# Dilated attention heads of a transformer kernel: outputs stored in two parts instead of one

## The chip, the cores and the metric

The kernel runs on one core of a Trainium2 chip. The metric is the device time of one execution in microseconds. Engines are named as the profile names them: PE is the matrix engine (TensorE), PEld its weight loads, DVE is VectorE, ACT is ScalarE, POOL is GpSimd, SP is SyncE. L902 is line 902 of the kernel.

## What is computed

A sequence of 1024 tokens with 1024 features goes through two blocks. The first block has a convolution layer and then a dilated attention layer, each with an adaptive normalisation ahead and a gated residual behind; the second has a sparse attention layer (indexer, top 256 of the keys, latent keys and values) and a convolutional feed-forward layer. The change lies in the dilated attention layer:

```python
def dilated_mixer(h, w_in, w_out, cos, sin):
    q, k, v, z = jnp.split(h @ w_in, [G * E, 2 * G * E, 2 * G * E + E], axis=-1)
    ...
    for g in range(G):        # rates 1, 4, 16
        ...
        o, lse = banded_attention(to_strided(q[:, :, g], r)[:, :, :, None], ...)
    wts = jax.nn.softmax(jnp.stack(lses, axis=0), axis=0)
    o = jnp.sum(wts[..., None] * jnp.stack(outs, axis=0), axis=0)
    y = o.reshape(B, S, E).astype(h.dtype) * jax.nn.silu(z)
    return y @ w_out
```

There are 8 heads of 128 features; `y @ w_out` is the out-projection.

## The kernel before, in words

Everything lies transposed, features on the 128 partitions and tokens along the free dimension, in two chunks of 512 tokens (`CH(c)`). Every matmul operand is kept as two numbers: `hi`, the value rounded to the matmul type float32r, and `lo`, the rest. A product takes three matmuls (`mm3`, and `gemm` for a block of 128 features): hi x hi, hi x lo, lo x hi. `split` (L381 to L385) makes the two from a float32 tile: a copy on ACT (L384) and a subtraction on DVE, or on another engine if one is named (L385). `weight` (L364 to L379) loads a block of weights from DRAM (L376) and makes its two parts on ACT (L377) and POOL (L378) into a ring of three pairs (`wring`), or loads ready parts (L372). `weight_own` (L666 to L673) does the same with buffers of its own.

The SBUF is handed out by `Arena`: pages, each of which holds at a time either float32 buffers or buffers of the rounded type (`ar.new(n, True)`; `new2` gives a pair of these). `new` prefers the buffers that were freed longest ago. A buffer that was given back may be in use still; whoever writes it next waits for its last reader. Nearly all loads and stores go through one in-order queue, that of SP (`dma`). The order of instructions on each engine comes from a scheduler: it follows the program's order as a priority and moves an instruction ahead where its simulated timeline has an engine free.

The dilated layer runs the heads one after another (loop at L948). A head projects queries and keys for three rates (`block`, L754; `rotate`, L733 to L749, which reads the projections from PSUM on ACT, L736 and L737, and DVE, L740), loads its values (L972), projects the gate `z`, and calls `attend` (L758 to L911). In between, `later.go()` prepares weights of later layers: load, split, and store as two parts (L353 to L358). `attend` makes scores and exponentials (L774 to L797), brings the row maxima and sums of the rates together by an exchange through a DRAM buffer (stores L810 to L812, loads L815 and L819; a transposition L817; weights L827 to L847), transposes the weighted scores with PE (`turned`: L857, split at L859 and L860) and multiplies them with the values. At the end of a head, for each chunk, DVE adds the last part (L902) and multiplies by the gate (L903) into a buffer `y`. For heads 0 to 6 `y` is stored to the DRAM tensor `yscr` as float32 (L908). For head 7 it is split at once and stays in SBUF (`Yc`, L905 and L906).

After the heads, `load_y` (L999 to L1007) loads for a chunk the seven stored outputs (L1004) and splits each (L1006), the subtraction on DVE for even heads and on POOL for odd ones. `finish_layer1` runs the out-projection of a chunk (`outproj`, L675 to L691: eight blocks of weights `w1o`, each a `gemm` over the eight heads in order, then the residual loaded at L685 and added at L686), and the norms behind it. Block 3 of chunk 0 has weights of its own buffers (L668 to L670). The calls stand at L1067 to L1072: `load_y` of chunk 0, five blocks of its out-projection, `load_y` of chunk 1, the rest. The scheduler mixes these loads, splits and matmuls with the end of head 7.

`load_y` serves two other layers as well (sources `yscr2` and `gscr`); those are single DRAM tensors.

Of the kernel before, what the change touches and what calls it, by code (L numbers as in the profile page):

```python
# [15 lines left out]
S = 1024  # L16
# [184 lines left out]
def emit(tc, I, OUT):  # L201
# [9 lines left out]
    dma = nc.sync.dma_start  # L211
# [4 lines left out]
    with sp as sp, pp as pp, dp as dp:  # L216
# [11 lines left out]
        def dram(shape, dtype=F32):  # L228
            serial[0] += 1
            return dp.tile(list(shape), dtype, name=f"d{serial[0]}")  # L230
# [150 lines left out]
        def split(hi, lo, src, hi_buf_f=None, engine=None):  # L381

            n = src.shape[-1]
            A.activation(hi.r[:, :n], src, AF.Copy)  # L384
            (engine or V).tensor_sub(lo.r[:, :n], src, hi.f[:, :n])  # L385
# [22 lines left out]
        def new2(n=512):  # L408
            return ar.new(n, True), ar.new(n, True)
# [71 lines left out]
        CH = lambda c: slice(512 * c, 512 * c + 512)  # L481
# [44 lines left out]
        Y = [[None, None] for _ in range(8)]  # L526
# [200 lines left out]
            dma(mask1[i].f, I["mask1"][:, 768 * i:768 * i + 768])  # L727
        m0 = [mask1[0].f[:, 256 * i:256 * i + 256] for i in range(3)]
        m12 = [mask1[1].f[:, 384 * i:384 * i + 384] for i in range(2)]
        yscr = dram([8, 128, S])  # L730
        Yc = [[None, None] for _ in range(8)]

        def rotate(p, c, out):  # L733
# [24 lines left out]
        def attend(h, q, k, vs, sz):  # L758
# [122 lines left out]
            def banded(i):  # L881

                s0 = lambda J, kk: S0[J // 2].f[:, 256 * (J % 2) + 128 * kk:
                                                256 * (J % 2) + 128 * kk + 128]
                pt = turned([s0((i - 1) % 8, 1), s0(i, 0), s0(i + 1, 1), s0(i + 2, 0)])
                p = psum("ps")
                for a in range(2):
                    tl = slice(256 * a, 256 * a + 256)
                    mm3(p[:, tl], v0(i + 2 * a), tuple(v[:, tl] for v in rr(pt)), True, True)
                for b in pt:  # L890
                    b.free()
                return p
# [6 lines left out]
            for c in range(2):  # L899
                p = banded(4 * c + 1)  # L900
                y = ar.new(512)
                V.tensor_tensor(nj(y.f), nj(p), ov[:, 64 * c:64 * c + 64], op=OP.add)  # L902
                V.scalar_tensor_tensor(y.f, y.f, 0.5, sz.f[:, CH(c)], op0=OP.mult, op1=OP.mult)  # L903
                if h == HEADS - 1:
                    Yc[h][c] = new2()  # L905
                    split(*Yc[h][c], y.f)  # L906
                else:
                    dma(yscr[h, :, CH(c)], y.f)  # L908
                y.free()
            for b in [*vs[0], *vs[1], *S0, *S1, o12, sz]:  # L910
                b.free()  # L911

# [35 lines left out]
        for h in range(HEADS):  # L948
            q = [new2(S), new2(S), (ar.new(S),)]
            k = [new2(S + 128), new2(S), (ar.new(S),)]  # L950
# [3 lines left out]
            for g in range(3):  # L954
                for t, off, pad in ((q, 0, 0), (k, 24, 64)):
                    p = block(off + 8 * g + h)
                    later.go()
                    for c in range(2):
# [5 lines left out]
                        b = t[g]  # L964
# [13 lines left out]
            for c in range(2):  # L978
                A.activation(sz.f[:, CH(c)], p[c], AF.Tanh, scale=0.5)
                V.scalar_tensor_tensor(sz.f[:, CH(c)], sz.f[:, CH(c)], 1.0, p[c], op0=OP.add,  # L980
                                       op1=OP.mult)
            attend(h, q, k, vs, sz)
        later.finish()
        for b in rope + mask1:
# [14 lines left out]
        def load_y(src, Y, c):  # L999
            for k in range(len(Y)):  # L1000
                if Y[k][c] is not None:
                    continue
                y = ar.new(512)
                dma(y.f, src[k, :, CH(c)])  # L1004
                Y[k][c] = new2()
                split(*Y[k][c], y.f, engine=G if k % 2 else V)  # L1006
                y.free()  # L1007

        def finish_layer1(c):
# [54 lines left out]
            if c == 1:  # L1064
                spare.free()

        load_y(yscr, Yc, 0)  # L1067
        ends1 = [finish_layer1(c) for c in range(2)]
        take(ends1[0], 5)
        load_y(yscr, Yc, 1)  # L1070
        drive(ends1[0])
        take(ends1[1], 6)  # L1072
# [402 lines left out]
        def finish_dsa(c, rest=()):  # L1475
            load_y(yscr2, Y2, c)
            acc = ar.new(512)
            xs = []

            def each(k, x):  # L1480
                square_sum(acc, x.f, k)
                xs.append(x)

            drive(outproj(prepared["w2o"], Y2, c, mods[:, 64:72], XF, X3, each))
            free_h(Y2, c)
            with tc.issue_after(lastn[3].ins):
                for _ in rest:
                    pass
            norm_h(xs, acc, s3, mods[:, 72:80], H3, c)
# [182 lines left out]
```

## Time and profile before

| | us |
|---|---|
| median of 3 runs | 2719.55 |
| the runs | 2713.51, 2719.55, 2720.99 |
| the profiled execution | 2724.1 |
| its span, first to last instruction | 2722.3 |
| mean granted clock of PE | 0.981 |

The profile is one execution. In it PE is busy for 95% of the span, DVE for 56%, ACT for 41%, POOL for 37%. A wait is put down to the instruction that released it. A matmul's duration includes its pipelined end, so durations of a run of matmuls overlap. "x12" counts instructions in a merged row. The granted clock is 1.00 at 2.4 GHz and 0.5 at 1.2 GHz. The heads lie at about 600 to 1406 us; head 0's last output is made at 740 us, head 6's at 1329, head 7's at 1409; the out-projection is under way from about 1377.

### The profile page before, as it was taken

How to read it: one execution, taken by the hardware profiler on the slowest of the kernel's cores; microseconds unless marked ns; L12 is line 12 of the kernel's file. 1: busy time of each engine (PE TensorE's matmuls, PEld its weight loads, DVE VectorE, ACT ScalarE, POOL GpSimd, SP SyncE). 2: the span in 40 equal slices, each digit the busy share in tenths (PEclk: the TensorE clock that was granted, in tenths of full speed). 3: DMA queues.
4: the chain of work that ended last, by engine and by line, in shares of the span. 5: the costliest groups of instructions: out<-in, count | busy, mean ns of one | idle time of the engine just before them, and what ended most of it. 6: DMA issues, size and time to landing. Idle time of an engine off the chain costs nothing. (4 is left out here: it accounts for less than half of the span.)

```text
span 2722.3 us, 34072 instructions
## 1 busy us (share of the span) xinstructions
PE 2588.6 (95%) x12070; PEld 2136.3 (78%) x12070; DVE 1528.9 (56%) x3260; ACT 1128.4 (41%) x1940; POOL 1009.8 (37%) x770
## 2 busy tenths in 40 slices
PE   8998999899999999999989888999999989999998
PEld 7876888788888788888867666777788868888887
DVE  7687532423756656665676699999555450222311
ACT  4211333414545445545443657784444442111132
POOL 1122236506446446536546335213111165200153
PEclk9999999999999999999999999999999999999999
DMA  7477765565444344444335674786566853676642
GB/s 296 156 260 258 261 222 193 166 199 171 166 163 170 139 163 171 149 170 172 132 122 182 212 248 117 248 269 225 192 203 212 273 194 107 210 256 245 224 122 74
DMA packets 208582, 524.67 MB, mean 193 GB/s; under 512 B 22258, under 2 KB 82202, under 8 KB 192796
## 3 DMA queue, kind: packets, MB, share of 16 engines
q1 hardware_dynamic: 199052, 497.20, 53.3%
q0 software_dynamic: 9216, 25.17, 3.1%
q8 instruction: 95, 1.56, 0.2%
q14 instruction: 75, 0.61, 0.1%
q10 hardware_dynamic: 144, 0.14, 0.0%
HBM read 394.03 MB, written 129.97 MB: 192 GB/s over the span
## 5 line engine op out<-in xcount | busy, mean ns | idle before, releaser
L256 PE MATMUL p<-page,wring 128*128 128x512 f32 (+2 forms) x8586 | 2017.9, 393 | 42.2 <-DVE page L572 11.5
L256 PEld LDWEIGHTS p<-page,wring 128*128 128x128 f32 (+1 forms) x8586 | 1602.0, 189 | 388.5 <-issue 10.4
L256 PE MATMUL p<-page,page 128*128 128x512 f32 (+5 forms) x2816 | 578.2, 349 | 64.9 <-DVE page L860 12.6
L378 POOL TENSOR_TENSOR wring<-wraw,wring 128x1024 fp32r<-128x1024 f32 (+1 forms) x159 | 387.9, 2440 | 551.6 <-ACT wring L377 479.6
L256 PEld LDWEIGHTS p<-page,page 128*128 128x128 f32 (+1 forms) x2816 | 461.8, 197 | 151.4 <-issue 18.4
L377 ACT ACTIVATE wring<-wraw 128x1024 fp32r<-128x1024 f32 (+1 forms) x159 | 164.6, 1036 | 301.0 <-PE p L256 272.7
L385 POOL TENSOR_TENSOR page<-page,page 128x512 fp32r<-128x512 f32 (+1 forms) x87 | 131.3, 1518 | 394.5 <-ACT page L384 369.6
L384 ACT ACTIVATE page<-page 128x512 fp32r<-128x512 f32 (+1 forms) x136 | 86.7, 651 | 178.3 <-DMA page<-d 69.8
L738 POOL TENSOR_TENSOR page<-page,page 128x512 f32<-128x512 f32 x96 | 125.4, 1310 | 71.4 <-ACT page L737 69.5
L355 DVE TENSOR_TENSOR wraw<-wraw,page 128x1024 fp32r<-128x1024 f32 (+1 forms) x64 | 78.8, 1231 | 126.4 <-ACT page L354 122.2
L301 DVE SCALAR_TENSOR_TENSOR page<-page,page 128x1024 f32<-128x1024 f32 x88 | 126.2, 1436 | 40.2 <-DMA page<-wmod 39.9
L747 POOL TENSOR_TENSOR page<-page,page 128x512 fp32r<-128x512 f32 x64 | 103.7, 1622 | 61.8 <-ACT page L746 61.6
L354 ACT ACTIVATE page<-wraw 128x1024 fp32r<-128x1024 f32 (+1 forms) x64 | 67.4, 1053 | 142.8 <-DMA wraw<-w3i 40.9
L1544 DVE SCALAR_TENSOR_TENSOR page<-p,page,page 128x512 f32<-128x512 f32 (+1 forms) x17 | 12.2, 719 | 202.9 <-PE p L256 202.9
L740 DVE TENSOR_TENSOR page<-p,page 128x512 f32<-128x512 f32 x96 | 66.1, 689 | 78.5 <-ACT page L737 73.1
L745 DVE TENSOR_TENSOR page<-page 128x512 f32<-128x512 f32 x64 | 95.4, 1492 | 25.6 <-POOL page L738 25.6
L1268 ACT ACTIVATE page<-page,page 128x1024 bf16<-128x1024 f32 (+1 forms) x93 | 86.9, 934 | 39.7 <-DVE page L1291 35.7
L746 ACT ACTIVATE page<-page 128x512 fp32r<-128x512 f32 x64 | 57.2, 894 | 75.7 <-DVE page L745 75.5
L736 ACT ACTIVATE page<-p 64x512 f32<-64x512 f32 x96 | 57.3, 596 | 72.4 <-PE p L256 54.1
L686 DVE SCALAR_TENSOR_TENSOR page<-p,page,page 128x512 f32<-128x512 f32 x48 | 35.9, 748 | 90.4 <-PE p L256 89.9
L1511 ACT ACTIVATE page<-p 128x512 f32<-128x512 f32 x44 | 26.2, 596 | 142.2 <-PE p L256 142.2
L441 POOL TENSOR_TENSOR page<-page,page 128x512 f32<-128x512 f32 x38 | 50.3, 1323 | 89.8 <-ACT page L440 89.8
(215 smaller groups left out, 2344.7 us busy)
## 6 DMA issues: line engine op xcount, KB each, us to landing
wring<-d SPq DMA_DIRECT2D x122, 1024.0 KB, 5.4
d<-page SPq DMA_DIRECT2D x95, 512.0 KB, 2.7
page<-wmod SPq DMA_DIRECT2D x88, 512.0 KB, 4.6
d<-page SPq DMA_DIRECT2D x153, 256.0 KB, 3.7
d<-wraw SPq DMA_DIRECT2D x63, 512.0 KB, 2.8
page<-d SPq DMA_DIRECT2D x121, 256.0 KB, 3.5
wraw<-w1i SPq DMA_DIRECT2D x56, 512.0 KB, 3.3
wraw<-w3i SPq DMA_DIRECT2D x44, 512.0 KB, 4.1
```

The lines of the kernel that those rows point to most:

```text
L256: lastn["mm"] = T.matmul(out, lhsT=l, rhs=r, start=start, stop=stop)
L301: V.scalar_tensor_tensor(w.f, w.f, 1.0, sil[j // 6].f, op0=OP.mult, op1=OP.mult, accum_out=m)
L354: A.activation(hi.r[:, :n], raw.f[:, :n], AF.Copy)
L355: V.tensor_sub(raw.r[:, :n], raw.f[:, :n], hi.f[:, :n])
L377: A.activation(hi.r[:, :n], raw.f[:, :n], AF.Copy)
L378: (lo_engine or G).tensor_sub(lo.r[:, :n], raw.f[:, :n], hi.f[:, :n])
L384: A.activation(hi.r[:, :n], src, AF.Copy)
L385: (engine or V).tensor_sub(lo.r[:, :n], src, hi.f[:, :n])
L738: G.tensor_mul(sw.f, sw.f, rope[1].f[:, CH(c)])
L745: V.tensor_tensor(a.f, a.f, sw.f, op=OP.add)
L747: G.tensor_sub(out[1], shape(a.f), out[2])
L1268: A.activation(junk.b[:, 0:sc.n], sc.f, AF.Sign, scale=-1.0, bias=at, accum_out=one)
```

## The change

`yscr` becomes a list of two DRAM tensors. At the end of every head `y` is split (ACT and DVE) and given back at once; head 7 keeps its parts as before, heads 0 to 6 store both parts, each a transfer of 128 x 512 float32 (256 KB). `load_y`, when its source is a list, loads the two parts directly into a pair of rounded buffers and does no split. The other two uses of `load_y` are as before.

```diff
-        yscr = dram([8, 128, S])
+        yscr = [dram([8, 128, S]) for _ in range(2)]
...
                 V.scalar_tensor_tensor(y.f, y.f, 0.5, sz.f[:, CH(c)], op0=OP.mult, op1=OP.mult)
+                parts = new2()
+                split(*parts, y.f)
+                y.free()
                 if h == HEADS - 1:
-                    Yc[h][c] = new2()
-                    split(*Yc[h][c], y.f)
-                else:
-                    dma(yscr[h, :, CH(c)], y.f)
-                y.free()
+                    Yc[h][c] = parts
+                    continue
+                for b, out in zip(parts, yscr):
+                    dma(out[h, :, CH(c)], b.f)
+                    b.free()
...
         def load_y(src, Y, c):
             for k in range(len(Y)):
                 if Y[k][c] is not None:
+                    continue
+                if isinstance(src, list):
+                    Y[k][c] = new2()
+                    for b, part in zip(Y[k][c], src):
+                        dma(b.f, part[k, :, CH(c)])
                     continue
                 y = ar.new(512)
                 dma(y.f, src[k, :, CH(c)])
```

## Rows read from the trace of the kernel before

**Rows 1.** The page: busy time, share, instructions of each engine.

```profile
PE 2588.6 (95%) x12070; PEld 2136.3 (78%) x12070; DVE 1528.9 (56%) x3260; ACT 1128.4 (41%) x1940; POOL 1009.8 (37%) x770
```

**Rows 2.** Waits of PE from 700 to 1340: total us, times, longest.

```profile
PE p L256 <- DVE page L860: 10.8, 6, 4.4
PE p L256 <- DVE page L740: 7.1, 7, 1.0
```

**Rows 3.** Stretches: length, busy PE, PEld, DVE, ACT, POOL; clock, DMA share, GB/s.

```profile
742.00:811.00 69.00, 69.00 (x340) 57.96 (x340) 38.61 (x96) 34.60 (x68) 37.25 (x30) 1.00 0.45 157
...
1372.00:1418.00 46.00, 35.18 (x182) 27.71 (x181) 34.83 (x90) 21.61 (x50) 15.83 (x16) 0.93 0.42 139
1418.00:1450.00 32.00, 32.00 (x142) 26.48 (x143) 22.68 (x19) 11.80 (x15) 27.23 (x13) 1.00 0.31 107
```

**Rows 4.** Waits of PE from 1368 to 1425: total us, times, longest.

```profile
PE p L256 <- ACT page L384: 4.3, 3, 2.3
PE p L256 <- DVE page L860: 1.8, 2, 1.6
PE p L256 <- POOL page L670: 1.4, 1, 1.4
PE p L256 <- DVE page L793: 1.1, 1, 1.1
PE p L256 <- DVE page L385: 0.8, 1, 0.8
PE p L256 <- DVE page L896: 0.7, 1, 0.7
PE p L256 <- POOL page L385: 0.5, 1, 0.5
```

**Rows 5.** Timeline of PE: start, us, line, tiles, count, wait before.

```profile
1383.40 5.49 PE L256 MATMUL p<-page,wring 128*128 128x512 f32 x12 [0.55 <-POOL page L385]
...
1406.13 4.27 PE L256 MATMUL p<-page,wring 128*128 128x512 f32 x18
...
1417.83 0.96 PE L256 MATMUL p<-page,wring 128*128 128x512 f32 x3 [1.64 <-ACT page L384]
```

**Rows 6.** Splits from 1365 to 1425: ns min/median/max, first and last start.

```profile
L384 ACT ACTIVATE page<-page x16: 614/617/632, 1371.2 to 1417.1; 128x512 fp32r<-128x512 f32 x16
...
L385 DVE TENSOR_TENSOR page<-page,page x10: 680/692/2446, 1377.8 to 1417.8; 128x512 fp32r<-128x512 f32 x10
...
L385 POOL TENSOR_TENSOR page<-page,page x6: 1268/1510/1833, 1372.6 to 1413.9; 128x512 fp32r<-128x512 f32 x6
```

**Rows 7.** Waits of SP's queue from 700 to 1420: total us, times, longest.

```profile
SPq L908 <- DVE page L903: 22.9, 13, 10.3
...
SPq L1004 <- PE p L256: 10.7, 2, 8.5
```

**Rows 8.** Timeline of SP's queue: start, us, line, count of issues.

```profile
1376.18 2.28 SPq L1004 DMA_DIRECT2D page<-d  x4
...
1378.99 0.43 SPq L1004 DMA_DIRECT2D page<-d  x1
1379.52 0.38 SPq L810 DMA_DIRECT2D d<-page  x1
...
1407.84 6.97 SPq L1004 DMA_DIRECT2D page<-d  x5
```

**Rows 9.** DMA issues of the whole run: KB each, median us to landing.

```profile
page<-d SPq DMA_DIRECT2D x121, 256.0 KB, 3.5
...
page<-d SPq DMA_DIRECT2D x34, 512.0 KB, 3.8
```

**Rows 10.** Timeline of POOL: start, us, line, count, wait before.

```profile
1382.07 2.51 POOL L385 TENSOR_TENSOR page<-page,page 128x512 fp32r<-128x512 f32 x2 [0.58 <-ACT page L384]
```

**Rows 11.** One stretch, columns as in rows 3.

```profile
1370.00:1380.00 10.00, 7.47 (x51) 6.03 (x49) 9.53 (x40) 8.45 (x26) 6.28 (x8) 1.00 0.54 183
```

**Rows 12.** L815, the exchange's last load, all eight heads.

```profile
DMA to landing us min/median/max: 1.5/1.6/1.6
```

## The prediction

> **What bounds the kernel now.** I read the page's busy shares first, then a table of stretches, then who TensorE waited for, then the timeline at the places that this named, and last the DMA queue of SyncE. The shares say that TensorE (PE) is the bound: 2588.6 of the 2722.3 us of the span [rows 1]. So work that the change moves between VectorE (DVE), ScalarE (ACT) and GpSimd (POOL) is worth something only where PE stands still. The change touches two stages. In the first, the eight heads, PE stands still very little: from 700 to 1340 us it waited 10.8 us for the splits of transposed scores (L860) and 7.1 us for L740 [rows 2], and the stretch that follows a head's last output is full, 69.00 of 69.00 us from 742 to 811 [rows 3], up to the next head's wait for L860. In the second, from 1372 to 1418 us, PE is busy for 35.18 of 46 us at a mean granted clock of 0.93, and then full again from 1418 [rows 3]. There head 7 is finished, one serial chain of scores, an exchange of row statistics through DRAM, and transposes, and PE fills its pauses with out-projection matmuls of heads 0 to 6. These need the heads' outputs loaded and split.
>
> The waits of PE in that stretch add up to 10.6 us [rows 4]: 4.3 for the ACT halves of splits (L384), 0.8 and 0.5 for the DVE and POOL halves (L385), together 5.6 us that belong to the very splits the change takes away, and 5.0 us that belong to head 7 itself (L860, L793, L896) or to the weights of block 3 (L670). Beside the waits there is a clock loss: 12 matmuls from 1383.40 take 5.49 us, or 0.457 each, where 18 of the same shape from 1406.13 take 4.27, or 0.237 each [rows 5]; the granted clock was at its lower level (1.2 GHz), right after the longest of these waits, 2.3 us. That is 12 x 0.220 = 2.6 us.
>
> **The change part by part.**
>
> Removed, in load_y: 14 splits. Each is one ACT copy (0.617 us) and one subtraction, on DVE (0.692) for even heads and on POOL (1.510 in this stretch) for odd ones [rows 6]. That is 14 x 0.617 = 8.6 us of ACT, 8 x 0.692 = 5.5 of DVE, 6 x 1.510 = 9.1 of POOL. (Heads 0 to 6 have four even and three odd in each of two chunks, 8 and 6.) On PE's path lie at most the 5.6 us of waits above, and the 2.6 us of clock if PE stays busy. Not all of it will come: what is late next is the load itself. Of the 5.6, 1.6 is one late wait at 1417.83 [rows 5], when the loads of the second chunk are split in the middle of the first chunk's matmuls; I take it whole. The other 4.0 come at 1376 to 1384; there the pieces of the loads land at about the time of the splits, and I take half, 2.0. Of the clock I take half, 1.3.
>
> Also removed from head 7's chain: ACT and DVE are in-order queues, and two ACT copies and two DVE subtractions stand between the chain's own instructions from 1376 to 1380. Bound: 0 (they fill gaps of the chain) to 2 x 0.617 + 2 x 0.692 = 2.6 us. I take 1.0, nearer to nothing, since the exchange through DRAM, not ACT, is the longest link there.
>
> Added, in the heads: 14 splits on ACT and DVE, 8.6 us and 14 x 0.692 = 9.7 us, and 14 more stores. They follow L903, which the change leaves as it is. The cover is the full stretch after each head [rows 3]: DVE is busy for 38.61 of 69 us there and ACT for 34.60, so 1.4 and 1.2 us per head fit. I cost them at 0. If the cover were gone, all of it in series on PE would be 14 x (0.617 + 0.692) = 18.3 us; that is the upper end. A lower end below nothing I exclude, because nothing is removed in that stage.
>
> Added on SyncE's queue: 14 stores and 14 loads, about 0.4 us each to issue (0.38 and 0.43 in [rows 8]). The stores stand behind the split instead of behind L903. SyncE already waited 22.9 us for L903 at these stores, 10.3 at worst [rows 7], with the next weights queued behind; each head adds about 0.617 + 0.692 = 1.3 us to that wait. The weights are fetched ahead, since PE shows no wait for a weight load in the heads [rows 2], so 0; ends 0 and 7 x 1.3 = 9.2 us.
>
> The doubled loads: seven loads of the first chunk go out from 1356 to 1378, because they wait for buffers; SyncE stood 10.7 us for PE at two of them [rows 7], and the last four leave from 1376.18 to 1378.46 [rows 8]. Seven more at about 0.4 us each are 2.8 us of issue. A load then lands 3.5 us after its issue [rows 9], so the last part is there at about 1378.5 + 2.8 + 3.5 = 1384.8 if the buffers come free as now, just when the second of two POOL subtractions ends now (1382.07 + 2.51 = 1384.58 [rows 10]). This is why I take only half of the early waits. New buffers come only from pages of the rounded type now, and 32 of those are released when head 7 has made its last projection, at 1369; if the loads get these, they can leave up to 7 us earlier, and the other half comes as well.
>
> Here a row and a rule can be weighed. The four loads from 1376.18 overlap: issued about 0.4 us apart, they still land within the 3.5 us median. So the second part of a pair costs one issue, 0.4 us. The Trainium skill (DMA: Bandwidth & Descriptors, Rules for kernel authors) asks for transfers of 1 MiB or more, because small ones pay their fixed part each; a pair of quarter-MB loads is against that. By that rule taken strictly a pair would land 3.5 + 3.5 us after its issue, 3.1 later than I say, and the sum below would be -2.8 us; the trace speaks for overlap, since a load of 512 KB lands in 3.8 us and one of 256 KB in 3.5 [rows 9].
>
> **The sum.** -1.6 - 2.0 - 1.3 - 1.0 + 0 + 0 = -5.9, about -6 us. The profiled execution took 2724.1 us (span 2722.3, 1.8 around it), so 2718.1 in its own terms. It lies 4.6 us above the median of the runs, 2719.55; there the forecast is 2713.5. A measurement of this kernel can tell a difference of about 0.3% from none, 8.2 us: faster is below 2711.4, slower above 2727.7.
>
> **The rivals.**
>
> More is gained. The loads take the buffers released at 1369, all parts are in place by 1378, PE runs on without a pause, keeps its clock, and head 7's chain ends earlier on freed queues. Bound: all waits and the clock, 10.6 + 2.6 = 13.2 us. For it: 63 out-projection matmuls (3 blocks x 7 heads x 3, 14.9 us at 0.237) are there to fill with, more than the waits. Against it: 5.0 us of the waits have nothing to do with the splits. At -8.5 to -13, centre -11: 2708.5.
>
> Nothing is gained. PE waits for landings where it waited for ACT, and the order that the scheduler finds (it is written anew for the whole program) takes the rest elsewhere. For it: SyncE's waits for buffers [rows 7]. 2719.5, plus or minus 3.
>
> Slower. The place is the exchange of head 7: its stores and loads of row statistics (a store at 1379.52 [rows 8]) share SyncE's queue and the DMA engines with the loads. From 1370 to 1380 the engines moved 183 GB/s at a share of 0.54 [rows 11], so 339 GB/s if full. If 26 loads (6.8 MB, both chunks) go out from 1372.7 ahead of the exchange, they take 20.1 us, to 1392.8, and the exchange comes 13.3 us later than 1379.5. To cover it there are the 18 fill matmuls that now come after head 7's last own ones, 4.3 us [rows 5], so PE stands 9.0 us more, and loses once more the 2.6 us that the lower clock cost after a pause; only the late 1.6 of the removed waits is left to set against it: 9.0 + 2.6 - 1.6 = +10, 2729.5. It decides from about 13 loads ahead of the exchange (3.4 MB, 10 us, against 4.3 covered and 5.6 removed). For it: loads of the second chunk already stand among the exchange's issues (one at 1378.99 [rows 8]). Against it: most of them go out only from 1407.84 [rows 8], and the last load of the exchange lands within 1.6 us in all eight heads, head 7 with its loads among them [rows 12]. The Trainium skill (DMA: Bandwidth & Descriptors, Queues, rings and completion order) says that what one issuing engine sends is consumed in ring order on each DMA engine, which is what this rival needs; no row here shows an exchange held up by loads.
>
> **How the numbers follow.** Forecast 0.38 (-3 to -9, so a sixth of it past 8.2), more gained 0.34, nothing 0.10, slower 0.18. Faster: 0.34 + 0.06 = 0.40. Same: 0.32 + 0.10 = 0.42. Slower: 0.18. The likeliest case's own range is 2710.5 to 2716.5. The range with 8 in 10 goes from 2704 (the gain of 13.2, and 2 us of run spread) to 2727, where nothing is gained and 7.5 of the 9.2 us on SyncE's queue are paid; the slower rival beyond it is the 2 in 10 left out.
>
> **What would show it.** Right: in the changed kernel no L384 or L385 works on a load of y before 1420; PE busy from 1372 to the solid stretch rises above 35.18 of 46 us, with the end of that stretch 5 to 7 us earlier; no lower clock there; the heads' full stretches stay full; ACT and DVE subtractions appear behind L903. Wrong: PE waits for a DMA landing in 1372 to 1390; L810 to L815 issue later than 1379 to 1384 as counted from the last projection matmul of head 7; or PE's waits for L740 or L860 in the heads exceed 17.9 us together.

## The result, and the profile after

The changed kernel takes 2739.26 us (median of 5 runs, 2737.31 to 2747.47) against 2719.55 for the kernel before in the same job: the medians are 19.7 us (0.7%) apart, and the ratio of the runs is 1.009 on record, interval 1.0071 to 1.0109. It is slower by 0.7 to 1.1%. The forecast was 2713.5, with a range up to 2727.

PE does the same 12070 matmuls as in [rows 1], in 5.7 us more of busy time and 7.6 us more of idle time (the profiled execution took 2737.31 us, that of the kernel before 2724.1, so these two are 13.2 us apart):

```profile
PE 2594.3 (95%) x12070; PEld 2142.6 (78%) x12070; DVE 1525.0 (56%) x3266; ACT 1125.7 (41%) x1942; POOL 1002.8 (37%) x764
```

To see where, I cut the span at events that both kernels have: the last output of head 0 (end of L902), that of head 6, the last residual of the out-projection (L686) and the last one of the sparse attention layer. Each row is a stretch with the columns of [rows 3]: the heads, the end of head 7 with the out-projection, the sparse attention layer, the rest. The kernel before:

```profile
738.86:1326.50 587.64, 570.76 (x2894) 482.70 (x2892) 372.02 (x777) 296.94 (x533) 306.25 (x236) 0.99 0.46 161
1326.50:1540.77 214.27, 201.44 (x941) 162.91 (x939) 135.57 (x222) 94.35 (x163) 110.73 (x69) 0.98 0.46 155
1540.77:2213.53 672.76, 622.20 (x2930) 507.18 (x2929) 500.88 (x1428) 376.68 (x718) 186.36 (x228) 0.98 0.67 223
2213.53:2722.30 508.77, 489.39 (x2194) 403.78 (x2192) 124.64 (x187) 119.19 (x169) 155.36 (x88) 0.98 0.53 175
```

The changed kernel:

```profile
737.39:1340.27 602.88, 575.73 (x2894) 487.16 (x2892) 379.91 (x789) 300.17 (x545) 310.22 (x236) 0.98 0.46 161
1340.27:1548.36 208.09, 196.57 (x928) 160.30 (x927) 128.39 (x216) 85.62 (x148) 101.24 (x63) 0.99 0.53 177
1548.36:2225.29 676.93, 628.57 (x2935) 511.82 (x2934) 500.24 (x1429) 380.45 (x724) 184.61 (x228) 0.97 0.67 223
2225.29:2735.60 510.31, 488.43 (x2201) 403.36 (x2199) 122.90 (x187) 118.54 (x168) 155.19 (x88) 0.98 0.53 174
```

The loss is in the heads, where PE has the same 2894 matmuls: 15.2 us longer. The out-projection is 6.2 us shorter, though it also has 13 matmuls fewer, nearly all of which stand in later stretches; at 0.237 us each [rows 5] that is 3.1 of it. In the heads PE waits for the splits of transposed scores, 18.3 us where [rows 2] has 10.8, and for a landing that it did not wait for at all (waits of PE from 700 to 1360, columns as there):

```profile
PE p L256 <- DVE page L860: 18.3, 7, 4.5
PE p L256 <- DVE page L740: 7.1, 7, 1.0
PE p L817 <- DMA page<-d: 2.5, 2, 1.4
```

The stretch after a head's last output, full in [rows 3], now has the wait for that landing in it (67.59 of 69 us from 740.50 to 809.50). More is lost at the pause that ends it. The same 70 us around this pause, in the kernel before, then in the changed one:

```profile
759.00:829.00 70.00, 66.82 (x349) 56.41 (x348) 40.21 (x100) 31.77 (x61) 29.57 (x24) 1.00 0.48 167
```

```profile
759.00:829.00 70.00, 63.28 (x314) 53.72 (x313) 39.02 (x96) 29.07 (x56) 27.02 (x22) 0.95 0.45 159
```

Look at the pause closely. First the timeline of the changed kernel (start, us, engine, line, count, wait before), DVE, POOL and PE around 812 us:

```profile
810.67 4.27 DVE L841 TENSOR_SCALAR page<-page,page 128x256 f32<-128x256 f32 x8
...
812.19 2.34 POOL L378 TENSOR_TENSOR wring<-wraw,wring 128x1024 fp32r<-128x1024 f32 x1 [11.71 <-ACT wring L377]
...
811.03 0.28 PE L256 MATMUL p<-page,page 128*128 128x256 f32 x1
815.59 1.01 PE L256 MATMUL p<-page,page 128*128 128x256 f32 x3 [4.29 <-DVE page L860]
816.40 1.05 PE L857 MATMUL p<-page,page 128*128 128x128 f32 x4
817.11 4.44 PE L256 MATMUL p<-page,page 128*128 128x256 f32 x20
...
823.44 2.79 PE L256 MATMUL p<-page,wring 128*128 128x512 f32 x11 [1.02 <-DVE page L740]
```

The same place in the kernel before:

```profile
810.61 2.19 DVE L841 TENSOR_SCALAR page<-page,page 128x256 f32<-128x256 f32 x8
...
812.18 2.87 POOL L378 TENSOR_TENSOR wring<-wraw,wring 128x1024 fp32r<-128x1024 f32 x1 [10.24 <-ACT wring L377]
...
811.02 0.28 PE L256 MATMUL p<-page,page 128*128 128x256 f32 x1
813.46 0.63 PE L256 MATMUL p<-page,page 128*128 128x256 f32 x3 [2.16 <-DVE page L860]
813.92 0.60 PE L857 MATMUL p<-page,page 128*128 128x128 f32 x4
814.27 2.88 PE L256 MATMUL p<-page,page 128*128 128x256 f32 x20
...
819.05 5.05 PE L256 MATMUL p<-page,wring 128*128 128x512 f32 x21 [1.02 <-DVE page L740]
```

Neither L841 (eight scalings on DVE) nor L378 (the subtraction of a weight block on POOL) is part of the change. Yet the eight scalings take 4.27 us instead of 2.19: one of them, the seventh, lasts 2.43 us where the others last 0.35, until just after POOL's subtraction is over (814.68 us against 814.53). PE's wait grows from 2.16 to 4.29, and the 20 matmuls behind it take 4.44 us instead of 2.88: after the longer wait the granted clock is at its lower level (1.2 GHz), as the stretch from 815 to 820 us of the changed kernel shows (columns of [rows 3]):

```profile
815.00:820.00 5.00, 4.41 (x20) 4.41 (x21) 3.12 (x5) 0.60 (x1) 0.00 (x0) 0.50 0.50 175
```

At 811 us both kernels stood at the same matmul; at the wait for L740 the changed one is 4.4 us behind. In this profile it happens in heads 1, 2 and 3; in the profile of before in head 2 alone.

The out-projection, answering to [rows 4]: the waits of PE from 1385 to 1442.

```profile
PE p L256 <- DMA page<-d: 4.2, 4, 2.3
PE p L256 <- ACT page L669: 2.6, 1, 2.6
PE p L256 <- DVE page L860: 2.0, 1, 2.0
```

The stretch that answers to the one from 1372 to 1418 in [rows 3]:

```profile
1390.00:1436.00 46.00, 37.29 (x196) 30.81 (x195) 25.28 (x70) 16.25 (x32) 9.92 (x10) 0.96 0.61 198
```

All waits for splits of loads (L384, L385) are gone; 4.2 us for the landing of the loads themselves stand in their place. What this gains is best read at one and the same place, a run of 126 matmuls that both kernels have behind the fill, with 421 or 422 matmuls between head 6's last output and its start. The kernel before, then the changed one:

```profile
1423.41 28.72 PE L256 MATMUL p<-page,wring 128*128 128x512 f32 x126
```

```profile
1433.70 28.72 PE L256 MATMUL p<-page,wring 128*128 128x512 f32 x126
```

From head 6's last output (1326.50 and 1340.27) that is 96.9 us before and 93.4 after: 3.5 us gained. In the second profiles, below, it is 96.2 and 93.8, so 2.9 us in the mean.

### The profile page after: what moved, and what is told of

It reads as the page before. It is cut to its first block, busy times and chain, and to the rows that moved or that the text cites. A ratio compares the mean times of both kernels' runs of the same rounds, so it can differ in the third digit from the quotient of the medians.

```text
span 2735.6 us, 34114 instructions
## 1 busy us (share of the span) xinstructions
PE 2594.3 (95%) x12070; PEld 2142.6 (78%) x12070; DVE 1525.0 (56%) x3266; ACT 1125.7 (41%) x1942; POOL 1002.8 (37%) x764
## 5 line engine op out<-in xcount | busy, mean ns | idle before, releaser
L256 PE MATMUL p<-page,page 128*128 128x512 f32 (+5 forms) x2811 | 592.9, 355 | 67.3 <-DVE page L860 20.3
L256 PEld LDWEIGHTS p<-page,page 128*128 128x128 f32 (+1 forms) x2811 | 473.8, 202 | 152.2 <-DVE page L860 23.3
L378 POOL TENSOR_TENSOR wring<-wraw,wring 128x1024 fp32r<-128x1024 f32 (+1 forms) x159 | 386.6, 2433 | 548.3 <-ACT wring L377 519.9
L377 ACT ACTIVATE wring<-wraw 128x1024 fp32r<-128x1024 f32 (+1 forms) x159 | 164.1, 1035 | 274.1 <-PE p L256 247.1
L385 POOL TENSOR_TENSOR page<-page,page 128x512 fp32r<-128x512 f32 (+1 forms) x81 | 123.1, 1528 | 369.5 <-ACT page L384 362.7
L384 ACT ACTIVATE page<-page 128x512 fp32r<-128x512 f32 (+1 forms) x136 | 87.2, 653 | 179.9 <-DMA page<-d 72.1
L301 DVE SCALAR_TENSOR_TENSOR page<-page,page 128x1024 f32<-128x1024 f32 x88 | 124.8, 1420 | 36.9 <-DMA page<-wmod 36.5
L740 DVE TENSOR_TENSOR page<-p,page 128x512 f32<-128x512 f32 x96 | 66.0, 688 | 65.9 <-ACT page L737 60.5
L745 DVE TENSOR_TENSOR page<-page 128x512 f32<-128x512 f32 x64 | 85.1, 1329 | 21.9 <-POOL page L738 21.9
L1386 POOL TENSOR_TENSOR page<-page,page 128x256 f32<-128x256 f32 x64 | 48.7, 770 | 115.0 <-DVE page L1406 58.5
L686 DVE SCALAR_TENSOR_TENSOR page<-p,page,page 128x512 f32<-128x512 f32 x48 | 35.6, 747 | 87.6 <-PE p L256 80.9
L1525 DVE TENSOR_SCALAR page<-page,page 128x512 f32<-128x512 f32 x44 | 25.6, 582 | 104.1 <-ACT page L1519 104.1
```

The costliest lines, as they stand in the source:

```text
L256: lastn["mm"] = T.matmul(out, lhsT=l, rhs=r, start=start, stop=stop)
L301: V.scalar_tensor_tensor(w.f, w.f, 1.0, sil[j // 6].f, op0=OP.mult, op1=OP.mult, accum_out=m)
L377: A.activation(hi.r[:, :n], raw.f[:, :n], AF.Copy)
L378: (lo_engine or G).tensor_sub(lo.r[:, :n], raw.f[:, :n], hi.f[:, :n])
L745: V.tensor_tensor(a.f, a.f, sw.f, op=OP.add)
```

## The experiments

**The two kernels once more**, with no edit, for a second profile of each.

> The kernel before, profiled once more. Two theories of the 20 us that the change costs. Port theory: the added splits fit into the heads, but they shift ACT against DVE by some 0.05 to 0.1 us, and so the subtraction of a weight block on POOL (L378) starts earlier after the first of the eight scalings of scores on DVE (L841). In the profiles so far L841 stood still for 2.1 us wherever L378 started 1.34 to 1.52 us after it, and never from 1.57 us on: one head of three before, three of three after; PE waits behind it (L860), and its clock falls behind the longer waits. Work theory: the splits themselves lie on the path of every head, 1.3 us per chunk. Port theory expects here that the stalls of L841 in heads 1 to 3 again go by the start of L378 (a threshold near 1.55 us), their number between 0 and 3 and the time with it, 5 to 6 us each. The work theory says nothing of it.

> The changed kernel, profiled once more. Port theory: heads 1 to 3 again with L378 at 1.3 to 1.6 us after L841 begins, stalled where it is below about 1.55; a head without the stall is shorter by 2 us and by up to 3.4 us of clock. Work theory: every head is longer than before by about the same amount, stalled or not.

Measured: before 2709.49 us, with no long scaling in any head; after 2735.22, with long ones in heads 1, 2 and 4. The stretches, both profiles of each kernel:

| stretch | before | after | difference of the means |
|---|---|---|---|
| up to head 0's last output | 738.9, 733.0 | 737.4, 735.3 | +0.4 |
| heads | 587.6, 577.6 | 602.9, 599.0 | +18.4 |
| end of head 7 and out-projection | 214.3, 214.0 | 208.1, 210.8 | -4.7 |
| sparse attention layer | 672.8, 672.2 | 676.9, 678.0 | +5.0 |
| the rest | 508.8, 510.9 | 510.3, 510.3 | +0.5 |

The sum, 19.6, is the difference of the medians, 19.7. The second profile of the kernel before has no long scaling in any head, as the port theory allows. The threshold near 1.55 us does not hold: in the changed kernel's head 4 a scaling is long with L378 starting 1.78 us after the first.

Two profiles of one kernel also give the price of a long scaling with no edit at all: the same head of the same program, from the last output of the head ahead of it to its own, with a long one and without. Before, head 2: 102.56 and 98.25 us; changed, head 3: 101.56 and 98.26; changed, head 4: 101.45 and 97.00. That is 4.3, 3.3 and 4.5 us, 4.0 in the mean.

So the heads are to be explained first, and 5 us behind the out-projection that no step of the forecast had.

**Each half of the change alone.** The heads as changed, with load_y as before:

```diff
-        load_y(yscr, Yc, 0)
+        load_y(yscr[0], Yc, 0)
...
-        load_y(yscr, Yc, 1)
+        load_y(yscr[0], Yc, 1)
```

> The heads as changed (split, two stores); the out-projection loads the first part alone as float32 and splits it as before. This leaves out the second parts of heads 0 to 6. Port theory and work theory: the loss of the heads is all here, without the gain of the out-projection: +18 to +25 us against before, heads 15 us longer. If the loss came from the doubled loads or from the later layers instead, this is within 3 us of before.

The heads as before, with load_y loading the stored output into both buffers of a pair:

```diff
-        load_y(yscr, Yc, 0)
+        load_y([yscr, yscr], Yc, 0)
...
-        load_y(yscr, Yc, 1)
+        load_y([yscr, yscr], Yc, 1)
```

> The heads as before (one float32 store); the out-projection loads that tensor twice, straight into the two parts, and splits nothing. This leaves out the split (both parts hold the whole value). Both theories: heads as before, the out-projection's start quicker by 4 to 8 us as forecast, so -4 to -8 us; if the doubled loads get in the way of head 7's exchange, +5 or more.

Measured, against the kernel before on the same chip (2713.38): stores alone 2723.81, ratio 1.0046 (1.0029 to 1.0064); loads alone 2717.33, 1.002 (1.0006 to 1.0034). The heads' stretch is 602.1 us with the stores alone, three long scalings among them, and 578.2 with the loads alone, with none. The heads' loss thus belongs to the split and the stores. Both times missed what was expected: +10.4 us with the stores alone, where +18 to +25 was expected (the seven runs spread from 2717.5 to 2732.2, and the profiled one is the slowest), and +4.0 with the loads alone instead of -4 to -8. The loads bring no gain to the whole here, and the sparse layer is 678.7 us long behind them, 664.0 behind the stores.

**Moving POOL's subtraction out of the way.** The ACT copy that releases L378 (L377, weight block of heads 1 to 7) is issued behind the fourth L859 of the head that runs then:

```diff
+            pin = turns[8 * (i % 8) - 5] if 17 <= i < 24 else None
+            with tc.issue_after(pin.ins) if pin else nullcontext():
+                w = weight(I["w1i"][i])
-            return gemm(weight(I["w1i"][i]), H, (0, 1), tag="po" if turn[0] % 2 == 0 else "mm")
+            return gemm(w, H, (0, 1), tag="po" if turn[0] % 2 == 0 else "mm")
...
-                A.activation(pt[0].r, p, AF.Copy)
+                turns.append(A.activation(pt[0].r, p, AF.Copy))
```

> The changed kernel, with one order added: in heads 1 to 7 the ACT copy of the weight block whose POOL subtraction met L841 is put behind the fourth ACT copy of transposed scores, so that L378 can't start before L841 is done. Nothing is computed otherwise. Port theory: no L841 of 2.4 us is left, PE's waits for L860 in the heads fall from 18.3 to below 10 us, the clock stays high there, and the time falls by 8 to 14 us against the changed kernel. Work theory: the stalls go, but each head is still longer by 1.3 us or more, so a gain of at most 3 us.

> The kernel before with the same added order. Port theory: one stall fewer, -3 to -6 us, and the changed kernel with the order is then within 4 us of this one or faster. Work theory: the changed kernel stays 12 us or more behind this one.

**Taking half of the scalings off DVE**, which leaves DVE through before POOL begins:

```diff
-                V.tensor_scalar(s, s, wgt[0].f[:, J:J + 1], None, op0=OP.mult)
+                if J % 2:
+                    A.activation(s, s, AF.Copy, scale=wgt[0].f[:, J:J + 1])
+                else:
+                    V.tensor_scalar(s, s, wgt[0].f[:, J:J + 1], None, op0=OP.mult)
```

> The changed kernel, with four of the eight scalings (L841) on ACT instead of DVE; the other four are done 1.1 us after the first, before L378 starts. Port theory: no stall left, -6 to -14 us against the changed kernel, less 1 us per head if ACT becomes the later one. Work theory: ACT has more to do, so no gain or a loss.

> The kernel before with four of the eight scalings on ACT. Port theory: one stall of DVE fewer, -6 to +2 us against before, and the changed kernel with the same edit within 5 us of it. Work theory: the changed kernel with the edit is 12 us or more behind this one.

Measured, beside 2714.13 for the kernel before: the changed kernel with the later copy 2719.27, ratio 1.0016 (1.0005 to 1.0028), and with half of the scalings on ACT 2716.77, 1.0014 (1.0001 to 1.0026). The kernel before with the later copy 2715.1, 0.9998 (0.9988 to 1.0008), and with the scalings on ACT 2701.21, 0.9951 (0.9938 to 0.9963). The timelines of the changed kernel, DVE and POOL in head 1, first with the later copy (L845 is L841 there), then with the scalings on ACT (L844):

```profile
806.80 2.18 DVE L845 TENSOR_SCALAR page<-page,page 128x256 f32<-128x256 f32 x8
...
812.40 2.37 POOL L378 TENSOR_TENSOR wring<-wraw,wring 128x1024 fp32r<-128x1024 f32 x1 [14.46 <-ACT wring L377]
```

```profile
809.48 1.13 DVE L844 TENSOR_SCALAR page<-page,page 128x256 f32<-128x256 f32 x4
...
812.49 2.40 POOL L378 TENSOR_TENSOR wring<-wraw,wring 128x1024 fp32r<-128x1024 f32 x1 [12.54 <-ACT wring L377]
```

In neither does L378 start while the scalings run, and no scaling is long in any head. The heads fall from 602.9 and 599.0 us to 585.5 and 583.4. With all of the change's work still in the heads, 15.5 and 17.6 us of the mean of 601.0 are gone. Three long scalings at 4.0 us are 12 of that. The rest is not theirs: neither edit touches the long scalings alone (the kernel before, with no long one, goes from 577.6 us to 574.5 with the scalings on ACT and to 583.0 with the later copy). That the long scalings are the largest single cause is shown from both sides: the one edit moves POOL, the other DVE.

They are not the whole. By the ratios the changed kernel gained about 20 us with either edit, more than the 14 expected at most. The kernel before gained nothing by the later copy, where 3 to 6 us were expected, and 12.9 us by the scalings on ACT, where 6 were expected at most. With the later copy in both, the two kernels are 4.2 us apart, about what the port theory named; with the scalings on ACT in both they are 15.6 apart, which is the sign of the work theory (12 or more).

**What is left in the heads.** With the scalings on ACT in both, the stretches of the kernel before:

```profile
734.31:1308.85 574.54, 567.30 (x2893) 479.05 (x2892) 363.05 (x752) 306.83 (x557) 306.96 (x236) 1.00 0.46 164
1308.85:1522.35 213.50, 201.95 (x941) 162.99 (x939) 135.18 (x219) 95.77 (x167) 110.23 (x69) 0.98 0.46 156
1522.35:2189.88 667.53, 620.60 (x2929) 505.36 (x2929) 500.17 (x1427) 383.82 (x724) 183.26 (x228) 0.98 0.67 225
```

and of the changed one:

```profile
736.86:1320.28 583.42, 569.63 (x2893) 478.97 (x2892) 366.92 (x764) 310.06 (x569) 310.40 (x236) 1.00 0.46 167
1320.28:1527.56 207.28, 195.31 (x928) 159.04 (x927) 128.19 (x211) 86.73 (x152) 101.61 (x63) 1.00 0.53 178
1527.56:2204.38 676.82, 626.90 (x2935) 511.89 (x2934) 498.19 (x1429) 381.30 (x724) 185.68 (x228) 0.97 0.67 223
```

So 8.9 us in the heads and 9.3 in the sparse layer are still open. The other pair gives less in the heads; with the later copy, the kernel before, then the changed one:

```profile
732.49:1315.46 582.97, 569.82 (x2894) 479.36 (x2893) 369.25 (x777) 295.05 (x533) 312.26 (x236) 1.00 0.45 162
```

```profile
734.86:1320.40 585.54, 570.25 (x2893) 482.11 (x2892) 369.75 (x788) 302.53 (x545) 313.90 (x236) 0.99 0.46 166
```

That is 2.6 us, a lower end, since the later copy itself makes the heads of the kernel before 5.4 us longer (577.6 to 583.0).

Seven more kernels, all with the scalings on ACT, ask for what is left in the heads and in the sparse layer. Four carry the change or part of it: the change for one chunk alone (the other stored once and split when loaded), the heads' work with load_y as before, and another priority at the out-projection. The edit for chunk 0 alone, against the changed kernel; that for chunk 1 has the numbers exchanged:

```diff
+                if h < HEADS - 1 and c != 0:
+                    dma(yscr[0][h, :, CH(c)], y.f)
+                    y.free()
+                    continue
                 parts = new2()
...
-        load_y(yscr, Yc, 1)
+        load_y(yscr[0], Yc, 1)
```

> The changed kernel with every second of the eight scalings of L841 on ACT, and the change for chunk 0 alone: chunk 1 is stored once as float32 and split when loaded, as before. Nothing of the computation is left out. Against the kernel before with the same scalings on ACT (2701.2 us) the whole change with them cost 15.6 us: 8.9 in the heads (from head 0's last output to head 6's, 574.5 to 583.4 us), -6.2 to the end of the out-projection with 13 matmuls fewer in it (3 us), 9.3 in the sparse attention layer behind it (667.5 to 676.8 us from the end of the out-projection to the end of that layer), 1 to 3 elsewhere. Theory R, the ready loads of chunk 1 lengthen the layer behind: this layer stays at 665 to 670 us here, the heads pay half of their 8.9, and the time is 2703 to 2707. Theory O, the scheduler writes the order of that layer anew in each kernel and its length has nothing to do with the loads: the layer falls anywhere from 664 to 679 us, the time anywhere from 2700 to 2717, and the chunk does not decide it.

> The same with the change for chunk 1 alone: chunk 0 is stored once as float32 and split when loaded. Nothing is left out. Theory R: the sparse attention layer takes 675 to 679 us, the heads pay half of 8.9, and the time is 2711 to 2716, so above the kernel with the change for chunk 0 alone by 8 or more. Theory O: the layer takes anything from 664 to 679, and the time lies from 2700 to 2717, with no fixed side to the other.

The heads' work alone has the edit of the stores alone; the other priority is this:

```diff
-        take(ends1[0], 5)
+        take(ends1[0], 6)
```

> The changed kernel with every second scaling of L841 on ACT, and load_y loads only the first part of each output as float32 and splits it (the second parts of heads 0 to 6 are left out). So the heads carry all of their new work, and the loads are those of the kernel before. The price of the new work in the heads without the stalls at L841: 8.9 us by the pair measured, so heads of 582 to 585 us from head 0's last output to head 6's; if the price came from something in the loads, the heads would be at 575 to 578. Theory R: the sparse attention layer takes 664 to 668 us, and the time is 2707 to 2711. Theory O: 664 to 679 us in that layer, 2707 to 2721.

> The changed kernel with every second scaling of L841 on ACT, and six blocks of chunk 0's out-projection in place of five before the loads of chunk 1 in the program's order: the same work with another priority of a few instructions. Nothing is left out. Theory R: the sparse attention layer stays at 675 to 679 us, and the time is 2714 to 2719, as with five blocks (2716.8). Theory O: a small nudge is enough to write the order anew; the layer moves by over 3 us to one side or the other, within 664 to 680, and the time with it, 2704 to 2720.

Measured, beside 2714.21 for the kernel before (stretches in us):

| kernel | time | ratio, interval | heads | out-projection, matmuls | sparse layer |
|---|---|---|---|---|---|
| chunk 0 alone | 2713.29 | 0.9996, 0.9983 to 1.0008 | 578.7 | 208.5, 928 | 676.6 |
| chunk 1 alone | 2716.9 | 1.0015, 1.0 to 1.0029 | 582.3 | 212.9, 933 | 672.7 |
| heads' work alone | 2718.47 | 1.0009, 0.999 to 1.0028 | 583.2 | 211.8, 928 | 671.2 |
| six blocks first | 2712.26 | 0.9993, 0.9978 to 1.0008 | 583.2 | 208.3, 928 | 675.4 |

Theory R (the ready loads of chunk 1 lengthen the layer behind) falls: the kernel with chunk 0 alone has the long layer, at 2713.29 where R had 2703 to 2707. Six blocks first, by itself, spoke for R: the layer moved by 1.4 us, not by over 3. The price in the heads is as expected, 583.2, and does not depend on the loads; it is not halved by a chunk (4.2 us with chunk 0 alone, 7.7 with chunk 1 alone). From head 6's last output to the run of 126 matmuls the heads' work alone takes 95.5 us and the whole change 92.5: the ready loads gain 3.0 us there. With chunk 0 alone it is 93.3, with chunk 1 alone 97.4, so the gain comes with chunk 0's loads.

**Splits or stores.** Both parts are made, one is stored:

```diff
-                for b, out in zip(parts, yscr):
-                    dma(out[h, :, CH(c)], b.f)
+                dma(yscr[0][h, :, CH(c)], parts[0].f)
+                for b in parts:
                     b.free()
```

> As the kernel that carries the heads' new work without the stalls (every second scaling of L841 on ACT, first part loaded and split again), but the heads store only the first of the two parts; the second is made and given back (so the second parts of heads 0 to 6 are left out). The heads there took 583.2 us from head 0's last output to head 6's, against 574.5 in the kernel before with the same scalings; PE waited 2.5 us more for the exchange's landing (L817), 2.0 more for L862 and 1.2 more for L863. Theory S, the doubled stores on SyncE's queue and the DMA engines are the price: without them the heads are at 576 to 579.5 us and the waits of L817 are gone. Theory P, the splits on ACT and DVE ahead of the next head's work are the price: the heads stay at 581.5 to 585, with the waits for L862 and L863 as they were. Time: 2708 to 2713 by S, 2713 to 2720 by P.

Measured: 2710.7 us, 0.9993 (0.9976 to 1.001); heads 578.3. Waits of PE in the heads, both parts stored, then one:

```profile
PE p L256 <- DVE page L740: 6.4, 7, 1.0
PE p L817 <- DMA page<-d: 2.5, 4, 1.0
PE p L256 <- ACT page L862: 2.3, 5, 0.7
PE p L256 <- DVE page L863: 2.0, 5, 0.4
```

```profile
PE p L256 <- DVE page L740: 6.1, 6, 1.0
PE p L256 <- DVE page L863: 4.0, 5, 1.1
```

The waits for the exchange's landing (L817) are gone, and 4.9 of the 8.7 us with them: theory S, as far as it goes. The other 3.7 are put down to the splits, which no run takes away by themselves. Nor are the 4.9 shown to be the transfer alone: with one store the scheduler also issued the exchange's store L811 ahead of a weight load (L376) that waits for its buffer, and with two behind it. In the kernel before with the same scalings L811 stands behind that load too, in heads 1 to 6, and PE never waits for L817; so that order does not make the waits by itself. The rest was not told apart.

**The sparse layer's order alone**, with no part of the change: six, then four blocks in the kernel before with the scalings on ACT.

```diff
-        take(ends1[0], 5)
+        take(ends1[0], 6)
```

> The kernel before with every second scaling of L841 on ACT, and six blocks of chunk 0's out-projection in place of five before the loads of chunk 1 in the program's order. No part of the change is in it and nothing is left out. It asks whether the sparse attention layer's length moves by the order alone. In the kernels measured so far that layer lost (waits of PE plus half of the time at the lower clock) 53 to 66 us without ready loads (six kernels) and 66 to 77 with them (seven). Theory O, the order alone: the nudge moves the layer's loss by over 3 us from the 60.6 of the kernel without it, and 67 or more is as possible as 55. Theory R, the ready loads: it stays between 53 and 66. Time: 2695 to 2715 by O, 2694 to 2707 by R.

> The same with four blocks in place of five. Theory O: the loss of the sparse attention layer moves by over 3 us from 60.6 to either side, up to 77. Theory R: it stays between 53 and 66. Time: 2695 to 2715 by O, 2694 to 2707 by R. If both of these kernels stay within 53 to 66, the ready loads are the likelier cause of the layer's loss; one of them above 67 says that the order alone can make it.

Measured: 2712.76 us, 0.9994 (0.9978 to 1.0009), and 2716.66, 1.0003 (0.9987 to 1.002), beside 2715.38. The sparse layer with six blocks, then with four:

```profile
1518.82:2201.21 682.39, 632.18 (x2941) 512.10 (x2939) 499.45 (x1429) 382.60 (x725) 184.91 (x228) 0.97 0.67 221
```

```profile
1523.26:2204.31 681.05, 629.90 (x2932) 510.57 (x2930) 497.52 (x1427) 379.30 (x721) 184.00 (x228) 0.97 0.66 221
```

PE's waits, 50.2 and 51.2 us, and half of the time at the lower clock make about 71 and 70, past the 67 that theory O asked for. A nudge that has nothing to do with the change lengthens this layer by 14.9 and 13.5 us over the 667.5 above. With ready loads it took 673 to 679 us, without them 664 to 682: no price of the loads can be read from it, only that the order is written anew by every edit.

## Why the prediction was wrong

**The step that failed** is "Added, in the heads ... I cost them at 0". Its cover was read by sums: DVE busy for 38.61 of 69 us and ACT for 34.60 [rows 3], so 1.4 us "fit". The sums leave out what a shift does at the one place where PE has nothing else to do, the wait for L860 [rows 2]. With the new work in the heads a scaling meets POOL's subtraction in three of heads 1 to 6 (9 of 18 in three profiles), without it in none or one (1 of 18); by what route the new work shifts the two was not traced. Each such meeting costs 3.3 to 4.5 us, more than the splits of a head in series would (2 x 1.3). Against the mean of the two profiles of before, 2.5 more of them at 4.0 are about 10 of the 18.4 us. The other 8 agree with the 8.9 of the pair with the scalings on ACT, which is the work itself; the other pair has 2.6, so this share is less sure. That the upper end of the term, 18.3 us, is about the truth is luck: it was worked out as "all of it in series on PE", and the splits are 3.7 of it.

**SyncE's queue**, 0 with the ends 0 and 9.2 us, cost up to 4.9. The reason given held: weights are fetched ahead, and PE waits for no weight load in the heads. What PE did wait for was the exchange (L817). SyncE's wait for the first store of a chunk rose from 22.9 us [rows 7] to this (waits of SyncE's queue from 715 to 1440), by 16.8 us where the upper end was 9.2: the prediction counted 1.3 us once per head, and a head has two such stores.

```profile
SPq L911 <- ACT page L384: 39.7, 14, 12.4
```

**The out-projection** had the right sign and place, and half of the size: -5.9 forecast, about -3 measured up to the run of 126 matmuls. No L384 works on a load of y before 1420. What came late next was the load, as the step said. The ready loads land 3.9 us after their issue in the median (2.7 to 7.1, where the profile has the landing), not 7.0, so the two of a pair overlap, as the prediction took it. Three of its signs failed: PE does wait for landings (4.2 us), there is a lower clock after the wait of 2.02 us at 1406.90 (mean 0.96 in that stretch), and the solid stretch comes about 3 us earlier, not 5 to 7. Busy time rose only from 35.18 to 37.29 of 46 us. The terms mis-sized are the waits. The forecast took 3.6 of the 5.6 us for splits as gain; all of these are gone, but 4.2 for landings stand in their place, and PE waits 2.6 us for block 3's weights (L669) where [rows 4] has 1.4 (L670).

**The rivals.** The slower one had the right sign at the wrong place: loads of y do not hold up head 7's exchange. Its store L810 leaves 10.6 us after head 7's last projection matmul, 10.3 in the kernel before, and what its load L819 brings is used 1.9 us after the issue. ([rows 12] says less than was read from it: the profile has the landing of L815 for three heads of eight, and head 7 is not among them.) The sign that did come was the last one named: PE's waits for L740 and L860 in the heads are 7.1 + 18.3 = 25.4 us, past the 17.9.

**The 5 us behind** were in no step. They are within what the order alone does to the sparse layer, so neither shown to be the change's nor excluded.

**A version that beats both** came of it: the kernel before with every second scaling on ACT, 2701.21 us. Its gain in the heads is sound, 574.5, 572.9 and 573.1 us in three kernels where the kernel before has 587.6 and 577.6. The rest of it rides on the order of the sparse layer, as the two nudged kernels show: with the same edit they are at 0.9994 and 1.0003 of the kernel before.

## What to carry to other kernels

Slack of an engine is to be read at the chain that the bound engine waits for, not as a sum over a stage: ask which instructions there would begin to overlap with which if one side moved by a microsecond or less. A pause of the matrix engine can cost more than itself: behind the wait of 4.29 us the clock was at its lower level, behind the one of 2.16 at the same place it was not. And where an order is written anew for the whole program, a nudge without meaning tells how much of a difference is order, before a story is made of it.

## What the runs showed of the hardware

That two engines block each other for a whole instruction was not in the forecast. Over heads 1 to 6 in six profiles with all scalings on DVE (36 heads), I took the start of L378 less that of the first scaling. Up to 1.52 us, all 7 heads have a scaling of 2.43 us; from 1.57 to 1.79, 3 of 8; from 2.04 on, none of 21. Counted from the first scaling, POOL's subtraction ends in the 15 heads up to 1.79 at 3.85 to 3.86 us where the seventh scaling is the long one, at 4.12 where the eighth is, and at 4.41 to 4.44 where none is: it gets in between two scalings, or only behind the last. It goes the other way as well: where DVE got through, POOL's subtraction took 2.87 us, in the rows above, instead of 2.34. In the two timelines of head 1 above, 50 ns of start time (1.52 us against 1.57) go with 2.1 us on DVE and 4.4 on PE. The runs of the kernel before spread from 2704 to 2727 us; none to two such heads would make up to 9 us of that, an estimate from the 3.3 to 4.5 above that no run shows by itself.

The Trainium skill (SBUF — State Buffer, Who interferes with whom) says that VectorE and GpSimd share a pair of SBUF ports as an exclusive lock: "Whoever issues first gets the shared pair for the whole instruction". The 2.43 us beside a subtraction of 2.34 to 2.55 agree with that. It names tensor_scalar among the forms that can take the pair; that the scalings were in such a mode no run here shows.
